# A fused linear layer with a low-rank update on one core: where three small software stores are issued, and which chunk's rows they carry

## The chip, the cores and the metric

The kernel runs on one core of one Trainium2 chip. The metric is the device time of a run in microseconds (us); the time of a kernel is the median of several runs. A profile is one execution, and its times count from the first instruction of its span.

## The reference

```python
x_flat = x.reshape(-1, in_dim)                 # x: 16 x 2048 x 256, so 32768 rows of 256
y = x_flat @ W                                 # W: 256 x 256
lora_out = x_flat @ lora_A                     # lora_A: 256 x 16
lora_out = lora_out * lora_E                   # lora_E: 16
lora_out = lora_out @ lora_B                   # lora_B: 16 x 256
y = y + scale * lora_out                       # scale = 1.0
return y.reshape(batch, seq_len, out_dim).astype(np.float32)
```

All inputs and the output are float32. The input x and the output y are 33.5 MB each. The low-rank factors can be multiplied out once, so that what is left is y = x (W + scale A E B).

## The kernel before

**Tiling.** The 32,768 rows are cut into 4 chunks of 8,192. A chunk lies in SBUF as 128 partitions x 64 rows x 256 columns: partition p of chunk c holds 64 rows that follow each other in memory, 64 KB. There are three homes for chunks (`home(c)`, L116), so chunk 3 uses the home of chunk 0. A result overwrites the input rows that it was computed from, and is stored from the same home.

**Groups.** The work goes by groups of 4 rows per partition: 16 groups in a chunk, 64 in all. Four engines pass each group on:

- GpSimd (POOL) casts 4 rows of a home to bf16 into `stage` (L191).
- TensorE (PE) transposes the stage, two bf16 taken as one fp32 word (`turn`, L242).
- VectorE (DVE) copies the transposed words from PSUM to `xt` (L226).
- PE multiplies by `weff`, the merged weight (`multiply`, L253).
- ScalarE (ACT) copies the product from PSUM back into the home (L207).

Stage, `xt` and both PSUM tiles have two buffers each. PE runs the loop of turn(i + 1) and multiply(i), so a turn runs one group ahead. After the last cast, GpSimd waits for the last turn but one, drains, and adds to one more stage semaphore (L193, L194), which releases the surplus turn at the end of PE's loop.

**Loads and stores.** `ORDER` (L18) lists by hand what SP issues, in order: "L" and "S" are a load and a store of rows s to e of a chunk. All of them go through SP's hardware queue (q1 in the profile). A store waits on `s_done`, which ACT raises behind a drain when a row group that ends a store is done (L210, L211). A load of chunk 3 waits until the store of chunk 0 has landed from the rows that it overwrites (L152).

**The shares.** One chunk, `SHARED`, has its first and last row in each partition left out of its hardware store. `share` (L161) stores these two rows, 1 KB each, from GpSimd's software queue (q0), in three DMAs, in the order of `SHARES` (L38): partitions 108 to 112 (5 of them, 10 KB), 0 to 107 (108, 216 KB) and 113 to 127 (15, 30 KB). Before the change SHARED is 1. The three DMAs raise one semaphore, `shared_stored`, and SP waits for all three at the end of its list (L159). That they may be issued is told by `s_shared`, which ACT raises behind a drain when it has written the last group of the shared chunk (L208, L209).

**The hold.** At chunk 2, row 16 (`HELD`, group 36), GpSimd does more than cast. First it waits for the load that brings these rows. Then it waits on `s_shared`, issues the three shares, and waits until the store of chunk 0, rows 0 to 39 (`HOLDERS`), has landed. Only then does cast 36 run.

**The end.** Behind SP's wait on L159 all engines meet in an exit barrier (L288, L324 in the profile), and after it SP waits for the three hardware stores (of chunks 1, 2 and 3) that nothing else waits for (`wait_for_stores`, L283; L284 in the profile).

Of the kernel before, what the change touches and what calls it, by code (L numbers as in the profile page):

```python
# [28 lines left out]
    ("S", 0, 40, 64),  # L29
    ("L", 3, 0, 32),  # L30
    ("L", 3, 32, 64),
    ("S", 1, 1, 63),
    ("S", 2, 0, 64),
    ("S", 3, 0, 64),
]

SHARED = 1
SHARES = (slice(108, 113), slice(0, 108), slice(113, P))  # L38

HELD = (2, 16)  # L40
# [14 lines left out]
def kernel(  # L55
# [45 lines left out]
    s_shared = sem("shared_done")  # L101
    shared_stored = sem("shared_stored")
# [13 lines left out]
    def home(c):  # L116
        return homes[c % N_HOMES]

    sync, gpsimd, scalar, vector, tensor = nc.sync, nc.gpsimd, nc.scalar, nc.vector, nc.tensor
# [41 lines left out]
    def share(engine, p, landed):  # L161
        first_and_last = (p, slice(0, ROWS, ROWS - 1))
        to, of = y_chunks[SHARED], home(SHARED)
        engine.dma_start(out=to[first_and_last], in_=of[first_and_last]).then_inc(landed, 16)  # L164

    def gpsimd_program():
        gpsimd.memset(ident[:], 0.0).then_inc(s_ident, 1)  # L167
        gpsimd.wait_ge(s_ident, 1)
        gpsimd.affine_select(  # L169
            out=ident[:],  # L170
            in_=ident[:],
            compare_op=ALU.not_equal,
            fill=1.0,
            base=0,
            pattern=[[-1, P]],
            channel_multiplier=1,
        ).then_inc(s_ident, 1)
        for g in range(N_GROUPS):
            c, b = g // GPC, g % GPC * CG
            for op, landed in loaded.items():  # L180
                if op[1:3] == (c, b):
                    gpsimd.wait_ge(landed, 16)
            if (c, b) == HELD:
                gpsimd.wait_ge(s_shared, 1)
                for p in SHARES:
                    share(gpsimd, p, shared_stored)
                for op in HOLDERS:
                    gpsimd.wait_ge(stored[op], 16)
            if g >= NS:
                gpsimd.wait_ge(s_turned, g - NS + 1)  # L190
            gpsimd.tensor_copy(out=stage[g % NS][:], in_=home(c)[:, b:b + CG, :]).then_inc(s_stage[g % UNROLL], 1)  # L191

        gpsimd.wait_ge(s_turned, N_GROUPS - NS + 1)  # L193
        gpsimd.drain().then_inc(s_stage[N_GROUPS % UNROLL], 1)  # L194

    def scalar_program():
        for name, to, of in (
            ("w", w_sb, W.rearrange("(q t) m -> q t m", t=KT)),
            ("b", b_sb, lora_B),
            ("e", e_sb, lora_E[:, None]),  # L200
        ):
            ins = scalar.dma_start(out=to[:], in_=of).then_inc(set_up_loaded[name], 16)
            opening.append(ins.ins.name)
        for g in range(N_GROUPS):
            c, b = g // GPC, g % GPC * CG
            scalar.wait_ge(s_y, g + 1)
            scalar.copy(out=home(c)[:, b:b + CG, :], in_=psum_y[g % NY][:]).then_inc(s_free[(g + NY) % UNROLL], 1)  # L207
            if (c, b + CG) == (SHARED, ROWS):  # L208
                scalar.drain().then_inc(s_shared, 1)  # L209
            if g in ends:  # L210
                scalar.drain().then_inc(s_done, 1)  # L211
# [76 lines left out]
    with tc.tile_critical(no_gpsimd_drain=True):  # L288
        sync_program()
        gpsimd_program()  # L290
        scalar_program()
        vector_program()
        tensor_program()
# [35 lines left out]
```

## Time and profile before

| what | value |
|---|---|
| median of 5 runs | 163.16 us (161.99 to 163.62) |
| the profiled execution | 161.78 us, its span 160.5 us |
| hardware queue q1 | 2304 packets, 66.86 MB |
| software queue q0 | 160 packets, 0.26 MB |
| GpSimd casts (L191) | 64 of 1040 ns |
| ACT copies (L207) | 64 of 1012 ns |
| GpSimd issues of a share (L164) | 3 of 674 ns |
| SP's issue of the last store | at 117.45 us |

How to read the profile: the page gives the busy time of each engine and its share of the span; then the span in 40 slices, one digit each, in tenths busy, with the load of the 16 DMA engines and their GB/s below; then the DMA queues with their packets and bytes. A line of a wait names who waited, for whom, and the us in total, the number of waits and the longest. A timeline line gives the start in us, the time taken, the engine, the line of the program, the operation and its tiles, and in brackets the idle time ahead of it and what ended it. The DMA view can be taken of a window: its 40 slices are then of that window, and the bytes of a packet are counted where it starts. SP's own work (issuing, waiting) is shown as SPq.

### The profile page before, as it was taken

How to read it: one execution, taken by the hardware profiler on the slowest of the kernel's cores; microseconds unless marked ns; L12 is line 12 of the kernel's file. 1: busy time of each engine (PE TensorE's matmuls, PEld its weight loads, DVE VectorE, ACT ScalarE, POOL GpSimd, SP SyncE). 2: the span in 40 equal slices, each digit the busy share in tenths (PEclk: the TensorE clock that was granted, in tenths of full speed). 3: DMA queues.
4: the chain of work that ended last, by engine and by line, in shares of the span. 5: the costliest groups of instructions: out<-in, count | busy, mean ns of one | idle time of the engine just before them, and what ended most of it. 6: DMA issues, size and time to landing. Idle time of an engine off the chain costs nothing.

```text
span 160.5 us, 2030 instructions
## 1 busy us (share of the span) xinstructions
PE 93.2 (58%) x782; PEld 81.9 (51%) x782; DVE 45.4 (28%) x66; ACT 66.1 (41%) x65; POOL 68.6 (43%) x73
## 2 busy tenths in 40 slices
PE   2979969959999990000999999999900000000000
PEld 1449958959999990000899989999800000000000
DVE  0155534525555550000255545555300000000000
ACT  3015775747777772000277777777720000000000
POOL 1527838377777734003577687687000000000000
PEclk9999999999999998555599999999995555555555
DMA  7999999999999997989999999979998998998993
GB/s 263 411 429 455 410 457 408 482 417 400 433 433 527 429 392 327 485 359 429 467 402 459 408 433 466 493 317 475 491 416 376 506 425 376 490 441 376 490 408 147
DMA packets 2675, 67.43 MB, mean 420 GB/s; under 512 B 528, under 2 KB 544, under 8 KB 752
## 3 DMA queue, kind: packets, MB, share of 16 engines
q1 hardware_dynamic: 2304, 66.86, 97.5%
q10 hardware_dynamic: 208, 0.28, 0.6%
q0 software_dynamic: 160, 0.26, 0.4%
q14 instruction: 3, 0.02, 0.0%
HBM read 33.85 MB, written 33.55 MB: 420 GB/s over the span
## 4 chain that ended last, share of the span: by engine, by line
DMA 42%; PE 26%; POOL 1%; ACT 1%; issue 1%; SPq 0%; ACTq 0%
DMA out_dram<-home 30%; PE psum_y L253 17%; DMA home<-in_x_dram 12%; PE psum_xt L242 9%; POOL stage L191 1%; ACT home L207 1%; SPq L153 0%; ACTq L211 0%; SPq L324 0%; SPq L288 0%
## 5 line engine op out<-in xcount | busy, mean ns | idle before, releaser
L207 ACT COPY home<-psum_y 128x1024 f32<-128x1024 f32 x64 | 64.8, 1012 | 49.3 <-PE psum_y L253 49.3
L191 POOL CAST stage<-home 128x1024 bf16<-128x1024 f32 x64 | 65.8, 1040 | 37.4 <-DMA home<-in_x_dram 14.5
L253 PE MATMUL psum_y<-weff,xt 128*128 128x256 bf16 x512 | 67.3, 275 | 0.0
L226 DVE COPY xt<-psum_xt 128x1024 bf16<-128x1024 bf16 x64 | 44.3, 692 | 61.8 <-PE psum_xt L242 61.8
L253 PEld LDWEIGHTS psum_y<-weff,xt 128*128 128x128 bf16 x512 | 50.7, 99 | 5.5
L242 PE MATMUL psum_xt<-ident,stage 128*128 128x128 f32 x260 | 40.8, 280 | 20.2 <-POOL stage L191 19.8
L242 PEld LDWEIGHTS psum_xt<-ident,stage 128*128 128x128 f32 x260 | 31.1, 144 | 23.1 <-issue 21.8
L266 PE MATMUL psum_y<-ident 128*128 128x512 f32 x4 | 3.8, 1101 | 2.9 <-POOL ident L169 2.9
L164 POOL DMA_DIRECT2D out_dram<-home x3 | 2.0, 674 | 4.5 <-DMA home<-in_x_dram 4.5
L266 PEld LDWEIGHTS psum_y<-ident 128*128 128x128 f32 x4 | 1.2, 323 | 3.9 <-POOL ident L169 2.9
L216 DVE TENSOR_SCALAR ate<-psum_y,e_sb 16x256 f32<-16x256 f32 x1 | 0.5, 472 | 7.2 <-PE psum_y L269 7.2
L207 ACT ACT_TABLE_LOAD x1 | 1.3, 1283 | 2.1 <-SPq L288 2.1
L275 PE MATMUL psum_y<-b_sb,ate 16*128 16x256 f32 x4 | 1.2, 416 | 0.0
L275 PEld LDWEIGHTS psum_y<-b_sb,ate 16*128 16x128 f32 x4 | 0.7, 202 | 0.4 <-issue 0.3
L167 POOL MEMSET ident<- 128x128 f32 x1 | 0.2, 204 | 1.7 <-SPq L288 1.7
L269 PEld LDWEIGHTS psum_y<-ident,a_sb 128*16 128x16 f32 x2 | 0.3, 137 | 1.2 <-issue 1.2
L230 DVE TENSOR_TENSOR weff<-w_sb,psum_y 128x512 bf16<-128x512 f32 x1 | 0.7, 689 | 0.5 <-PE psum_y L275 0.5
L269 PE MATMUL psum_y<-ident,a_sb 128*16 128x128 f32 x2 | 0.6, 421 | 0.0
L169 POOL TENSOR_SCALAR_AFFINE_SELECT ident<-ident 128x128 f32<-128x128 f32 x1 | 0.3, 283 | 0.2 <-POOL ident L167 0.2
L310 POOL MEMSET const-float32-0.0<- 128x1 f32 x1 | 0.1, 98 | 0.2 <-issue 0.2
L310 POOL MEMSET const-bfloat16-1.0<- 128x1 bf16 x1 | 0.1, 101 | 0.0
L310 POOL MEMSET const-uint8-127<- 128x1 uint8 x1 | 0.1, 101 | 0.0
(1 smaller groups left out, 0.1 us busy)
## 6 DMA issues: line engine op xcount, KB each, us to landing
home<-in_x_dram SPq DMA_DIRECT2D x4, 4096.0 KB, 24.8
out_dram<-home SPq DMA_DIRECT2D x1, 7936.0 KB, 38.6
home<-in_x_dram SPq DMA_DIRECT2D x3, 2048.0 KB, 13.2
home<-in_x_dram SPq DMA_DIRECT2D x1, 6144.0 KB, 57.3
out_dram<-home SPq DMA_DIRECT2D x1, 5120.0 KB, 48.1
home<-in_x_dram SPq DMA_DIRECT2D x1, 3072.0 KB, 20.0
out_dram<-home SPq DMA_DIRECT2D x1, 3072.0 KB, 46.2
home<-in_x_dram SPq DMA_DIRECT2D x1, 1024.0 KB, 5.3
```

The source lines that it names most:

```text
L164: engine.dma_start(out=to[first_and_last], in_=of[first_and_last]).then_inc(landed, 16)
L191: gpsimd.tensor_copy(out=stage[g % NS][:], in_=home(c)[:, b:b + CG, :]).then_inc(s_stage[g % UNROLL], 1)
L207: scalar.copy(out=home(c)[:, b:b + CG, :], in_=psum_y[g % NY][:]).then_inc(s_free[(g + NY) % UNROLL], 1)
L216: vector.tensor_scalar(out=ate[:], in0=psum_y[0][:R, :KT, :P], scalar1=e_sb[:], scalar2=float(scale), op0=ALU.mult, op1=ALU.mult,).then_in ...
L226: vector.tensor_copy(out=xt[g % NX][:], in_=psum_xt[g % NT][:].bitcast(BF16)).then_inc(s_xt[g % UNROLL], 1)
L230: vector.tensor_add(out=weff[:], in0=w_sb[:], in1=psum_y[1][:, :KT, :]).then_inc(s_free[0], 1)
L242: ins = tensor.transpose(psum_xt[i % NT][:, b, :], words[:, b, :], ident[:])
L253: ins = tensor.matmul(psum_y[i % NY][:, b, :], xt[i % NX][:, b, t::KT], weff[:, t, :], start=(t == 0), stop=(t == KT - 1),)
L266: tensor.matmul(psum_y[1][:, :2, :], ident[:], ident[:, None, :].to_broadcast([P, 4, P]), start=True, stop=True)
L269: ins = tensor.transpose(psum_y[0][:R, t, :P], a_sb[:, t, :], ident[:])
L275: ins = tensor.matmul(psum_y[1][:, t, :], ate[:, t, :], b_sb[:], start=True, stop=True)
L310: nc = _bacc.Bacc("TRN2", target_bir_lowering=False, num_devices=1)
```

## The change

The shared chunk becomes chunk 2. Chunk 1's hardware store carries all 64 rows of each partition, and chunk 2's rows 1 to 62. GpSimd no longer waits on `s_shared` and issues the shares in the hold ahead of cast 36; it does so after the last cast and after the drain that releases PE's last turn. At the hold the wait for the store of chunk 0 stays. ACT raises `s_shared` after the last group of chunk 2 (group 47) instead of chunk 1 (group 31), as L208 follows SHARED.

```diff
-    ("S", 1, 1, 63),
-    ("S", 2, 0, 64),
+    ("S", 1, 0, 64),
+    ("S", 2, 1, 63),
     ("S", 3, 0, 64),
 ]
 
-SHARED = 1
+SHARED = 2
 SHARES = (slice(108, 113), slice(0, 108), slice(113, P))
...
             if (c, b) == HELD:
-                gpsimd.wait_ge(s_shared, 1)
-                for p in SHARES:
-                    share(gpsimd, p, shared_stored)
                 for op in HOLDERS:
                     gpsimd.wait_ge(stored[op], 16)
...
         gpsimd.wait_ge(s_turned, N_GROUPS - NS + 1)
         gpsimd.drain().then_inc(s_stage[N_GROUPS % UNROLL], 1)
+        gpsimd.wait_ge(s_shared, 1)
+        for p in SHARES:
+            share(gpsimd, p, shared_stored)
```

## The prediction

> **What bounds the kernel now.** I read the page first for busy shares, then the slices, then the chain that ended last, then the waits of the issuing queues, then the DMA view in narrow windows around the two places that the change touches.
>
> ```profile
> span 160.5 us, 2030 instructions
> PE 93.2 (58%) x782; PEld 81.9 (51%) x782; DVE 45.4 (28%) x66; ACT 66.1 (41%) x65; POOL 68.6 (43%) x73
> POOL 1527838377777734003577687687000000000000
> DMA  7999999999999997989999999979998998998993
> q1 hardware_dynamic: 2304, 66.86, 97.5%
> q0 software_dynamic: 160, 0.26, 0.4%
> HBM read 33.85 MB, written 33.55 MB: 420 GB/s over the span
> ```
>
> No engine is busy for more than 58% of the span, and all of them stop three quarters of the way through, while the DMA line stays at 7 to 9 tenths until the last slice. The hardware queue's packets fill 97.5% of 16 engines' span. The 67.4 MB of traffic is the bound; what the shares carry is 0.26 MB of it. The waits of the queue on SP and of POOL show how little the engines' order decides:
>
> ```profile
> SPq L284 <- SPq L284: 41.0, 1, 41.0
> POOL stage L191 <- DMA out_dram<-home: 10.4, 1, 10.4
> POOL out_dram L164 <- DMA home<-in_x_dram: 4.5, 1, 4.5
> ```
>
> SP starts its last wait 41.0 us ahead of the end, at 119.4, when only stores are left. The last store was issued at 117.45 and took 0.33, so 1.65 us lie between it and this wait: the exit barrier. POOL's timeline shows the two idle stretches around the shares, and where its casts end:
>
> ```profile
> 62.49 2.02 POOL L164 DMA_DIRECT2D out_dram<-home  x3 [4.54 <-DMA home<-in_x_dram]
> 74.96 2.02 POOL L191 CAST stage<-home 128x1024 bf16<-128x1024 f32 x2 [10.45 <-DMA out_dram<-home]
> ...
> 111.60 1.04 POOL L191 CAST stage<-home 128x1024 bf16<-128x1024 f32 x1 [0.27 <-PE psum_xt L242]
> ```
>
> How long the shares take today, from the page's list of issues (last number: us from issue to landing), and the DMA view of 67.5 to 75, where their packets first appear (62.5 to 67.5 has none on q0):
>
> ```profile
> out_dram<-home POOLq DMA_DIRECT2D x1, 216.0 KB, 13.7
> out_dram<-home POOLq DMA_DIRECT2D x1, 30.0 KB, 14.9
> out_dram<-home POOLq DMA_DIRECT2D x1, 10.0 KB, 7.9
> ```
> ```profile
> q1 hardware_dynamic: 99, 3.09, 95.4%
> q0 software_dynamic: 99, 0.21, 7.1%
> ```
>
> Last, the DMA view of 155 to 160.5 in slices of 0.1375 us. A packet of 65,536 bytes in one slice reads 477 GB/s, so the line counts the starts of the last round of packets, one on each of the 16 engines:
>
> ```profile
> GB/s 0 477 0 0 0 0 0 0 953 1907 1430 953 477 477 0 477 477 0 0 477 0 0 0 0 0 0 0 0 0 0 0 0 0 0 0 0 0 0 0 0
> ```
>
> After the lone 477 at 155.2 (still the round before), the 16 starts lie between 156.1 and 157.7; their mean slice is number 11.2, the last is 19. The engine that ends last does so 7.8 slices, 1.07 us, after the mean one. That is all that a perfect balance at the end could give.
>
> **The change part by part.** The sum is made on the profiled execution (161.78 us, span 160.5), which lies 1.38 below the median of the five runs, 163.16; I carry the difference over.
>
> *The three issues leave the place ahead of cast 36* (chunk 2, row 16). They took 2.02 us on POOL, from 62.49 to 64.5. The cast behind them waits for the store of chunk 0's first 40 rows and starts at 74.96, so POOL stood idle for 10.4 us after them. Worth 0; the wait for that store is the cover, and without it 2.02 us of POOL would be gained. The wait for `s_shared` there goes too: ACT's drain for it (L209) started at 56.4 and took 1.04, so it was met before the load that POOL really waited for, at 62.49. Worth 0.
>
> *The share packets leave that store's time.* By 75, 0.21 of their 0.26 MB had been started. At the 423 GB/s of 62.5 to 74.9 that is 0.50 us by which the store may land earlier, and with it cast 36 and the issue of chunk 3's first load, both near 74.9. Neither sets the end: the load queues behind chunk 0's other store, and the last store, issued at 117.45, reaches the engines only when that of chunk 2 is through, 20.8 us of packets before the end (eight rounds of 2.42 plus the stagger), so at about 139. Late next is the queue itself. I take 0, bounds -0.5 and 0.
>
> *Two rows change places between the hardware stores.* Chunk 1's store grows from 7,936 to 8,192 KB, chunk 2's shrinks by the same. One ends 0.26 MB / 420 GB/s = 0.6 us later, the other then ends where it did. Both were issued well ahead (83.2 and 96.5). Net 0.
>
> *ACT's drain for `s_shared`* moves behind group 47, where L211 already drains (1.04). Two in a row cost 1.04 and 0.014 at the end of chunk 1 today, and one of each will stay. Net 0.
>
> *The shares now go out behind the last cast.* The cast ends at 112.64, the drain that releases PE's last turn comes before them (L194: 313 ns from 112.9, done at 113.2), and `s_shared` is long set. Three issues of 0.674 take until about 115.3. Nothing that computes is queued behind them on POOL; the exit barrier is. On SP, L159 now waits for their landing, with the exit barrier (1.65) and the last wait queued behind it, and the program's end behind that. So: when do they land? First packets came 5.0 us after the first issue: 118.2 now. From there to the last landing (63.9 + 14.9 = 78.8) were 11.3 us. Software packets took turns with hardware packets of 41 KB (1.97 MB in 48 packets of the window 62.5 to 67.5, 91.1% of 16 x 5 us: 1.52 each), later 24 KB ones of about 0.9: 4.6 turns of 1.6 to 74.9, then about 4 of 1.0, so nine turns. Now the packets beside them are of 63 to 66 KB: 263 of them in 118 to 160.5 at 93.5% of 16 x 42.5 us, 2.42 each, 2.5 with the software packet. Nine turns are 22.5 us: landing at about 141. With a third more turns it is 148. SP's last wait is released at 160.4; take 1.65 off for the barrier and 10 us are left at the worse of these. I take 0, bounds 0 and +3.3 (first rival).
>
> *The bytes on each engine* stay as they were: the three issues keep order and size. But 20 KB or so more on a late engine is 20 KB / 27 GB/s (65.5 KB in 2.42 us) = 0.76 us, and the order in which engines leave the last loads decides who is late. Bounds -1.07 (balanced) and +0.8; I take 0, as the total per engine is nearest to the row of before.
>
> A rule against the change, to be left out by whoever wants rows alone: the Trainium skill, "DMA: Bandwidth & Descriptors", gives about 2.0 us fixed for each software DMA (section "Anatomy of one DMA") and calls DMAs under 64 KB mostly overhead ("Rules for kernel authors"); two of these three are 10 and 30 KB. By it, estimated, three fixed costs at the open end would be +6 us, about 169; the rows above put the whole landing 10 us or more inside other transfers, and by them it is 0.
>
> Sum: 161.78 + 0 = 161.78, and 163.16 + 0, rounded **163.2 us**. A difference of about 1% (1.63 us) is what a measurement of this kernel can tell from no change; the five runs of before spread over 1.63.
>
> **The rivals.**
>
> *The shares land last (slower).* Place: L159 on SP. If each 1 KB row were a packet of its own, the 108-partition share would need 18 turns on an engine where 9 partitions go through it, and all three some 23: 118.2 + 23 x 2.5 = 175.7. It decides from (160.1 - 118.2) / 2.5 = 17 turns on. The price has a cap, as the last store leaves the engines at 160.1 and the rest then runs alone: six packets of up to 4 KB at 27 GB/s, 0.15 each, 0.9; 0.4 of landing as for the last store; 1.65 of barrier; near 3.3 with what is left between: 166.5. For it: every small packet has to wait behind a 2.42 us one. Against: 160 packets for 256 KB and 48 completions mean that rows travel together, and nine turns sufficed before.
>
> *The middle gets smoother and the end evener (faster).* The slices from 60.2 and 64.2 show 7 tenths and 327 to 485 GB/s around the old issue. Between 58.5 and 62.5 the rate is 360 against 420: 4 us x 60/420 = 0.6. If the shares caused that and went from the end's imbalance as well, 0.6 + 1.07 = 1.67: 161.5 us. Against: the dip starts before the first issue at 62.49, and 104 to 108, with no share near, shows 333.
>
> *The early landing carries through (no change still).* If the 0.5 us were kept to the end: 162.7.
>
> *The other order leaves the late engine later (no change still).* +0.8: 164.0.
>
> **How the numbers follow.** No change in the mean, in its three forms, 0.83: its own range is 163.2 - 1.07 to 163.2 + 0.8, 162.1 to 164.0. Shares landing last 0.06, and 0.04 for a late engine beyond 0.8 with a partial delay: slower 0.10. The smoother middle 0.05, and 0.02 for both bounds below at once: faster 0.07. The own range holds about 7 in 10; moved out to the 1% bounds on either side, 161.5 to 164.8, it holds a little over 8 in 10, and the first rival lies outside.
>
> **What would show it.** POOL: no L164 at 62.5, three at about 113.3, and an idle wait of about 12 us ahead of cast 36 for the store alone. DMA: no q0 packets at 67 to 79, all 160 between 118 and 141 (148 at most). SP: the last wait begins at about 142 instead of 119.4, and lasts about 18 us instead of 41. The store of chunk 0 lands up to 0.5 us earlier, with the last store's issue up to 0.5 earlier and the span's end unmoved. The prediction is wrong if SP's last wait is short or gone, if L159 ends after 158, or if the last round of packets is spread over much more or less than 1.6 us.

## The result and the profile after

| | before | after |
|---|---|---|
| median | 162.34 us (79 runs, 161.5 to 163.73) | 161.22 us (42 runs, 160.74 to 162.36) |
| profiled execution | 161.78 us, span 160.5 us | 161.13 us, span 159.8 us |

The ratio after to before is 0.9937, with a 95% interval of 0.9923 to 0.9951: the change saves 0.63%, 1.02 us of 162.34. (It is the ratio of the means, 161.34 to 162.37; that of the medians is 0.9931.) The median of before was 163.16 in the five runs that the prediction was made from, and is 162.34 over 79.

The page of the changed kernel, with the same lines as for before:

```profile
span 159.8 us, 2029 instructions
PE 94.5 (59%) x782; PEld 82.8 (52%) x782; DVE 45.4 (28%) x66; ACT 66.1 (41%) x65; POOL 68.9 (43%) x73
DMA  6999999999999997989999999979979979979976
q1 hardware_dynamic: 2304, 66.86, 97.9%
q0 software_dynamic: 160, 0.26, 0.4%
```

Packets and bytes are the same, and the DMA engines are still the bound. The waits of SP and POOL, and POOL's timeline:

```profile
SPq L144 <- DMA out_dram<-home: 22.3, 1, 22.3
SPq L284 <- SPq L284: 17.7, 1, 17.7
POOL stage L188 <- DMA out_dram<-home: 16.9, 1, 16.9
```
```profile
74.72 2.02 POOL L188 CAST stage<-home 128x1024 bf16<-128x1024 f32 x2 [16.85 <-DMA out_dram<-home]
...
114.03 2.02 POOL L164 DMA_DIRECT2D out_dram<-home  x3 [1.04 <-PE psum_xt L242]
```

The first line is SP at the end of its list, waiting for the shares (the wait of L159, which the view puts under L144): 22.3 us from 118.1 to 140.4. After the exit barrier it still waits 17.7 us for the last hardware store, so the shares do not set the end. Their landing, from the page's list of issues:

```profile
out_dram<-home POOLq DMA_DIRECT2D x1, 216.0 KB, 21.0
out_dram<-home POOLq DMA_DIRECT2D x1, 30.0 KB, 25.0
out_dram<-home POOLq DMA_DIRECT2D x1, 10.0 KB, 7.3
```

The software packets start between 119.5 and 140.1, in nine bursts about 2.4 us apart, which is the time of one of the 65,536-byte packets beside them (2.42 us).

The last round of packets, in the DMA view of 155 to 160.5 (477 GB/s is one packet's start in a slice of 0.1375 us):

```profile
GB/s 0 0 0 0 0 0 477 953 953 0 953 2860 953 0 477 0 0 0 0 0 0 0 0 0 0 0 0 0 0 0 0 0 0 0 0 0 0 0 0 0
```

The mean start is in slice 10.0, the last in 14: 0.55 us apart, where it was 1.07 before. In this pair of executions half a microsecond of the 0.65 is there. The experiments test whether the gain rests on that.

### The profile page after: what moved, and what is told of

It reads as the page before. It is cut to its first block, busy times and chain, and to the rows that moved or that the text cites. A ratio compares the mean times of both kernels' runs of the same rounds, so it can differ in the third digit from the quotient of the medians.

```text
span 159.8 us, 2029 instructions
## 1 busy us (share of the span) xinstructions
PE 94.5 (59%) x782; PEld 82.8 (52%) x782; DVE 45.4 (28%) x66; ACT 66.1 (41%) x65; POOL 68.9 (43%) x73
## 3 DMA queue, kind: packets, MB, share of 16 engines
q1 hardware_dynamic: 2304, 66.86, 97.9%
## 4 chain that ended last, share of the span: by engine, by line
DMA 42%; PE 26%; POOL 1%; ACT 1%; SPq 1%; issue 0%; ACTq 0%; POOLq 0%
DMA out_dram<-home 30%; PE psum_y L253 17%; DMA home<-in_x_dram 13%; PE psum_xt L242 9%; POOL stage L188 1%; ACT home L207 1%; SPq L153 0%; ACTq L211 0%; SPq L324 0%; POOLq L187 0%; SPq L288 0%
## 5 line engine op out<-in xcount | busy, mean ns | idle before, releaser
L253 PE MATMUL psum_y<-weff,xt 128*128 128x256 bf16 x512 | 69.0, 280 | 0.0
L253 PEld LDWEIGHTS psum_y<-weff,xt 128*128 128x128 bf16 x512 | 51.4, 100 | 6.3
```

The lines of the kernel that those rows point to most:

```text
L253: ins = tensor.matmul(psum_y[i % NY][:, b, :], xt[i % NX][:, b, t::KT], weff[:, t, :], start=(t == 0), stop=(t == KT - 1),)
```

## Where the packets take longer

Three views of the kernel before give a measure that the page's slices are too coarse for. First a calm stretch, 20 to 40, loads alone; then 79 to 83, where the engines go over from chunk 0's stores to chunk 3's loads; then 99 to 103, where they go over to chunk 1's store:

```profile
q1 hardware_dynamic: 304, 8.65, 100.2%
...
q1 hardware_dynamic: 79, 1.73, 102.9%
...
q1 hardware_dynamic: 50, 1.61, 100.4%
```

The last number is the time that the packets took, as a share of 16 engines in the window; a packet counts whole where it starts, so it can pass 100%. In the calm stretch that is 1.002 x 16 x 20 / 8.65 = 37.1 us of one engine per MB. At the first switch it is 38.1, at the second 39.9. Over what the bytes take at the calm rate (37.06 before rounding), the two windows cost each engine 0.11 and 0.29 us. The same two windows of the changed kernel:

```profile
q1 hardware_dynamic: 77, 1.76, 102.4%
...
q1 hardware_dynamic: 49, 1.74, 105.9%
```

That is 37.2 and 39.0 us per MB, 0.02 and 0.21 us. I call the sum of both the excess at the switches (before 0.40, after 0.23) and give it for the runs below, as one profile of each can say only so much.

A longer packet at a change of direction is not in itself a sign of the shares. The change from loads to chunk 0's stores, in the window 58 to 76, first for before and then for after, has more of it than either switch:

```profile
q1 hardware_dynamic: 211, 6.89, 92.4%
...
q1 hardware_dynamic: 223, 7.18, 97.2%
```

That is 38.6 and 39.0 us per MB, an excess of 0.67 and 0.87 us: as much without early shares as with them, so it is left out of the sum.

## The experiments

Every run was timed beside runs of the kernel before on the same chip. Four theories come up: A, the shares even out the end (it takes four engines to get 4 KB of shares, twelve to get 20 KB, and the four to be late; the profile does not name the engine of a packet, so this was not seen); B or E, software packets early in the run cost by themselves; C, the choice of rows matters; D, engines put apart ahead of the switches cost. N, that software packets close ahead of the first switch cost, came later.

**Place alone.** The shares stay with chunk 1.

```diff
             if (c, b) == HELD:
-                gpsimd.wait_ge(s_shared, 1)
-                for p in SHARES:
-                    share(gpsimd, p, shared_stored)
...
         gpsimd.drain().then_inc(s_stage[N_GROUPS % UNROLL], 1)
+        gpsimd.wait_ge(s_shared, 1)
+        for p in SHARES:
+            share(gpsimd, p, shared_stored)
```

> The shares stay with chunk 1's rows, and only their place moves behind the last cast. Theory A (balance: the shares give 4 of the 16 DMA engines about 4 KB and 12 of them 20 KB; given behind the last loads, the 4 light ones are those that are late by then, so the last round ends more evenly): ratio to before 0.994, last round of packets spread over about 1.1 us as after the change instead of 1.5. Theory B (what is saved is the early place itself, in the hold and beside chunk 0's stores): 0.994 too. Theory C (which chunk's rows go through the software queue is what counts): 1.000.

Measured: 0.9942 (0.991 to 0.9975), excess 0.05. C is out: the gain is in the place. But the last packet started about 1.0 us behind the mean one, as in before, and the gain was there all the same.

**No shares at all.**

```diff
-    ("S", 1, 1, 63),
+    ("S", 1, 0, 64),
...
-        sync.wait_ge(shared_stored, 16 * len(SHARES))
...
-                gpsimd.wait_ge(s_shared, 1)
-                for p in SHARES:
-                    share(gpsimd, p, shared_stored)
```

> No software stores at all: the hardware stores of chunks 1 and 2 carry all 64 rows. Theory A: without the relief the late engines stay late by the 16 KB (0.6 us) that the light ones are spared, so no better than before: 0.999 to 1.004, and the last packet starts 1 us or more after the mean one. Theory B: nothing early is left to pay for, 0.994. Theory C: 1.000.

Measured: 0.9952 (0.9922 to 0.9982), excess 0.11. Its last round, in the same window and slices as above:

```profile
GB/s 0 0 0 0 0 1430 953 0 1907 477 953 0 0 1430 0 477 0 0 0 0 0 0 0 477 0 0 0 0 0 0 0 0 0 0 0 0 0 0 0 0
```

One engine starts last in slice 23, 1.8 us behind the mean of the round. This execution took 162.32, more than the kernel's median of 161.75, so its uneven end may well have cost it something. The ratio is what speaks against A, which had 0.999 to 1.004: without any shares the kernel is 0.5% faster, so those of before were not worth having, and A is out as the main cause. What shares in the late place give on top, 0.9937 against 0.9952, is inside the intervals.

**Late, with another four engines light.**

```diff
 SHARED = 2
-SHARES = (slice(108, 113), slice(0, 108), slice(113, P))
+SHARES = (slice(113, P), slice(0, 108), slice(108, 113))
```

> As after the change, but the shares of 15 and 5 partitions change places in the order of issue (15, 108, 5), which should put the 4 light engines elsewhere among the 16. Theory A: the late engines now get 20 KB instead of 4, 0.6 us more, so most of the gain goes: 0.998 to 1.002, the spread of the last round 1.5 us or more. Theory B and C: 0.994, as after the change.

Measured: 0.9951 (0.9922 to 0.9979), excess 0.05. B's number, 0.994, is inside the interval; A's range begins at 0.998, just outside it.

**Issued ahead of chunk 3's first cast**, chunk 1's rows.

```diff
+            if (c, b) == (3, 0):
+                gpsimd.wait_ge(s_shared, 1)
+                for p in SHARES:
+                    share(gpsimd, p, shared_stored)
             if (c, b) == HELD:
-                gpsimd.wait_ge(s_shared, 1)
-                for p in SHARES:
-                    share(gpsimd, p, shared_stored)
```

> Chunk 1's rows, issued ahead of chunk 3's first cast (near 93 us), so that the first software packets start near 98, at the end of the last loads (their last round starts near 99 to 100.7). Theory A: most turns still come after the last loads: 0.995, between 0.993 and 0.998. Theory B, if the hold and chunk 0's stores are what the early place costs: 0.994; if it is being ahead of the last loads: 0.997 to 1.000.

Measured: 0.9917 (0.9887 to 0.9948), excess 0.08. No cost in this place either.

**The old place, even shares.**

```diff
-SHARES = (slice(108, 113), slice(0, 108), slice(113, P))
+SHARES = (slice(0, P),)
```

> The place of before (in the hold, chunk 1's rows), but one software DMA of all 128 partitions, 16 KB on every engine, instead of 4 KB on four and 20 KB on twelve. Theory D (the uneven bytes, put ahead of the last loads, leave the engines staggered there, which costs 0.5 to 1 us by the end): 0.994, like the kernel without shares. Theory E (software packets early in the run cost by themselves, wherever they fall among the engines): 1.000. Theory A (balance at the end) would give 0.999 to 1.004.

Measured: 0.9973 (0.9944 to 1.0001), excess 0.16. Between D and E: the interval just misses D's 0.994 and just holds E's 1.000.

**The old place, twice the shares.** `share` takes the rows as an argument; chunk 1's hardware store is left with rows 2 to 61.

```diff
-    ("S", 1, 1, 63),
+    ("S", 1, 2, 62),
...
-                for p in SHARES:
-                    share(gpsimd, p, shared_stored)
+                for rows in (slice(0, ROWS, ROWS - 1), slice(1, ROWS - 1, ROWS - 3)):
+                    for p in SHARES:
+                        share(gpsimd, p, shared_stored, rows)
```

> The place of before, but four rows of each partition (0, 1, 62, 63) through the software queue in six DMAs: 8 KB on the four light engines, 40 KB on the other twelve, 1.2 us apart. Theory D: the cost doubles, 1.004 to 1.008. Theory E, if it is the turns of the software queue: 1.004 to 1.006; if it is one fixed cost: 1.000. If the early shares are harmless: 1.000 or below.

Measured: 1.0041 (1.0016 to 1.0067). Its two windows, 79 to 83 and 99 to 103:

```profile
q1 hardware_dynamic: 68, 1.42, 92.0%
...
q1 hardware_dynamic: 54, 1.73, 116.0%
```

41.5 and 42.9 us per MB: an excess of 0.39 and 0.63, 1.02 in all. More early shares, more time, and more of it at the switches.

**The same place in the code, behind the wait for the store.**

```diff
             if (c, b) == HELD:
+                for op in HOLDERS:
+                    gpsimd.wait_ge(stored[op], 16)
                 gpsimd.wait_ge(s_shared, 1)
                 for p in SHARES:
                     share(gpsimd, p, shared_stored)
-                for op in HOLDERS:
-                    gpsimd.wait_ge(stored[op], 16)
```

> Chunk 1's rows, the three shares issued after the wait for chunk 0's store instead of ahead of it, so near 74.7; cast 36 starts 2.0 us later, with some 20 us of slack behind it. The software packets take their turns from 80 on, beside the end of chunk 0's second store and the first load of chunk 3, still ahead of the last loads. Theory D: 1.000, as the stagger is still there before the last loads. Theory E, if it is the issue at the change from loads to stores near 62 that costs: 0.994.

Measured: 0.9944 (0.9919 to 0.9968), excess 0.07. POOL issued the shares at 75.58 instead of 62.49, and cast 36 came 2.0 us behind them:

```profile
75.58 2.02 POOL L164 DMA_DIRECT2D out_dram<-home  x3 [17.39 <-DMA out_dram<-home]
77.59 2.03 POOL L191 CAST stage<-home 128x1024 bf16<-128x1024 f32 x2
```

Thirteen microseconds of delay, the same bytes, the same engines, and the whole gain. It also shows that the 2.02 us on POOL, now uncovered, cost nothing. The windows of 79 to 83 and 99 to 103:

```profile
q1 hardware_dynamic: 74, 1.67, 97.4%
...
q1 hardware_dynamic: 51, 1.67, 97.7%
```

37.3 and 37.4 us per MB, next to nothing beyond the calm rate.

**The kernel before, once more.**

> The kernel before, once more, as a second profile of it and as a measure of how far two sets of runs of one program differ: 1.000, within 0.003.

Measured: 1.0006 (0.9978 to 1.0034), excess 0.40 again.

**The early rows by the hardware queue, uneven and even.** SP issues them between chunk 0's second store and chunk 3's first load; GpSimd issues none.

```diff
-SHARES = (slice(108, 113), slice(0, 108), slice(113, P))
+SHARES = (slice(0, 108), slice(108, P))
...
             kind, c, s, e = op
+            if op == ("L", 3, 0, 32):
+                sync.wait_ge(s_done, 3)
+                for p in SHARES:
+                    share(sync, p, shared_stored)
```

> The first and last rows of chunk 1 go out early, but through SP's hardware queue, between chunk 0's second store and chunk 3's first load, as two DMAs of 108 and 20 partitions. If 108 partitions go by 12 engines and 20 by 10, the engines are left 18 to 22 KB (0.7 to 0.8 us) apart from the four that get none, just ahead of the switch from stores to loads. Theory D (the stagger ahead of the switch is what costs): 1.000, from 0.998 to 1.004. Theory E (software packets early): 0.994 to 0.996.

Measured: 0.9963 (0.9937 to 0.9988), excess at the second switch 0.07 (the first window holds the 1 KB rows themselves, so it is not comparable). The two DMAs left 22 completions in the trace (2,582 packets on the hardware queue against 2,304, of which 256 are the rows), where the even form below left 16; 12 and 10 engines, as expected, would leave 22.

The even form has `SHARES = (slice(0, P),)`.

> The same place and queue as the hardware run with two DMAs, but one DMA of all 128 partitions, 16 KB on each engine. Theory D: 0.995, like the kernel without shares. Theory E: 0.995 as well. If rows of 1 KB cost ahead of the switch however they are issued: 1.000.

Measured: 0.9939 (0.991 to 0.9968), excess at the second switch 0.19. The intervals of the two overlap. D's 1.000 is outside that of the uneven one, the lower end of its range, 0.998, inside: rows that should put the engines apart just ahead of the switch cost less than the software shares of before, if anything.

**The old place, twice the shares, even**: the doubled run with `SHARES = (slice(0, P),)`.

> The place of before, four rows of each partition through the software queue as in the doubled run, but as two DMAs of 128 partitions, 32 KB on each engine. Theory D: 0.995 to 0.998, as the engines are not moved apart. Theory E (software turns early in the run): 1.002 to 1.005, close to the doubled run with uneven shares (1.0041).

Measured: 0.9971 (0.9947 to 0.9996), excess 0.61. Even shares in the old place give the same time, once or twice, within these intervals. So here the time follows neither the number of turns nor the excess (0.16 and 0.61).

**The old place, another four engines light**: before with `SHARES = (slice(113, P), slice(0, 108), slice(108, 113))`.

> The place of before, with the shares of 15 and 5 partitions exchanged in the order of issue, so that another four engines are the light ones. Theory D in its plain form (any four engines 16 KB ahead of the others at the switch): 1.000. If it matters that the light ones of before are late by something else: 0.996 to 0.998, or 1.003, as the others are nearer to or farther from the rest. Theory E: 1.000.

Measured: 1.0008 (0.9981 to 1.0034), excess 0.84. The order of issue, and with it which engines should be light, makes no difference to the time that these runs can tell.

**Earlier and later within the hold.** Issued ahead of the wait for chunk 2's second load:

```diff
+            if (c, b) == HELD:
+                gpsimd.wait_ge(s_shared, 1)
+                for p in SHARES:
+                    share(gpsimd, p, shared_stored)
             for op, landed in loaded.items():
                 if op[1:3] == (c, b):
                     gpsimd.wait_ge(landed, 16)
             if (c, b) == HELD:
-                gpsimd.wait_ge(s_shared, 1)
-                for p in SHARES:
-                    share(gpsimd, p, shared_stored)
```

> As before, but the three shares are issued ahead of the wait for chunk 2's second load, near 58 instead of 62.5, so that their packets (from 63 to about 75) are through some 5 us ahead of the switch from stores to loads at 80, with the engines just as far apart. Theory D (engines apart at the switch): 1.000. Theory N (software packets in the last few us ahead of the switch lengthen the packets at it): 0.994 to 0.996.

Measured: 0.9976 (0.9946 to 1.0005), excess 0.80. The last software packet started at 76.5.

And about 6 us later, behind five more casts of group 36, which only let time go by:

```diff
                 gpsimd.wait_ge(s_shared, 1)
+                gpsimd.wait_ge(s_turned, g - NS + 1)
+                for again in range(5):
+                    gpsimd.tensor_copy(out=stage[g % NS][:], in_=home(c)[:, b:b + CG, :]).then_inc(s_again, 1)
+                    gpsimd.wait_ge(s_again, again + 1)
                 for p in SHARES:
```

> As before, but GpSimd first casts group 36 five times more (about 6 us, only to pass time, in its idle stretch), so that the shares are issued near 68.7 and their packets run from about 73.7 to 85, across the switch at 80. Theory D: between the place of before and that behind the hold, 0.997 to 1.000. Theory N: 1.000 or above.

Measured: 0.9988 (0.9958 to 1.0019), excess 0.40. Issued at 68.64, with packets from 73.1 to 82.2. Neither place is clear of before's 1.000, and the intervals of the two overlap. That of the early one also reaches down to N's 0.996, and that of the late one holds N's 1.000. So the times do not decide about N. The excess does not either, as it differs between executions: the three profiles of 161.8 to 162.1 us (before, before again, at 68) have 0.40 each, the two of 162.9 and 163.0 (at 58, other engines) 0.80 and 0.84, and the ratios of before and of the other engines are the same.

**Twice the shares, behind the wait for the store**: the doubled run with the order of the run behind the wait.

> Four rows of each partition, uneven as in the doubled run, issued behind the wait for chunk 0's store. Theory D: the switch from stores to loads is past, but the engines are 32 KB (1.2 us) apart at the last switch near 100: 0.996 to 1.000. Theory N: software packets beside loads are harmless at twice the number too: 0.994.

Measured: 0.995 (0.992 to 0.9979), excess 0.12. In the place behind the wait even the double amount costs nothing that these runs can tell.

**Twice the shares, behind the last cast**: the changed kernel with rows 0, 1, 62 and 63.

```diff
-    ("S", 2, 1, 63),
+    ("S", 2, 2, 62),
...
+        for rows in (slice(0, ROWS, ROWS - 1), slice(1, ROWS - 1, ROWS - 3)):
+            for p in SHARES:
+                share(gpsimd, p, shared_stored, rows)
```

> The changed kernel with four rows of each partition of chunk 2 (0, 1, 62, 63) issued behind the last cast. Theory A in a weak form (the light engines are late by about one share): 0.994 to 0.998, as two shares make the other twelve late. If the light engines are late by more than one share: 0.991. Theories D and N: 0.994, as nothing follows but stores.

Measured: 1.009 (1.0055 to 1.0125), so 1.009 / 0.9937 = 1.5% or 2.5 us above the changed kernel. No theory had expected this. SP's waits and the end of the chain say why:

```profile
SPq L144 <- DMA out_dram<-home: 41.8, 1, 41.8
```
```profile
113.72 0.05 POOLq L191
113.77 0.75 issue
114.52 3.91 POOL out_dram L164 x6
```

The last wait for the hardware stores is gone from the list; SP waits 41.8 us for the shares, to about 160.4, and the exit barrier comes behind that, to a span of 162.4. The shares now land last. This is the prediction's first rival, brought about by twice the turns.

**The two best again, side by side.** First the kernel with the shares ahead of chunk 3's first cast, then the changed kernel.

> The kernel with chunk 1's shares issued ahead of chunk 3's first cast, run again beside the changed kernel, since it had the lowest ratio so far (0.9917, against 0.9937 of the change). If the place beside the last loads is better than that behind the last cast: 0.992, and 0.002 or more below the changed kernel of the same runs. If it is only one of the places that come after the costly stretch: 0.994, within 0.002 of it.

Measured: 0.9926 (0.9903 to 0.9949), excess 0.09.

> The changed kernel again, as the measure for the run beside it and as its second profile: 0.994. In the trace, packets beyond their usual time at the two switches near 80 and 100 add up to under 0.3 us per engine, as in every run without early software packets so far.

Measured: 0.9934 (0.9901 to 0.9967), excess 0.11. 0.0008 apart, so the same: no version was found that beats the changed kernel.

**What the runs say together.**

| software packets | runs: ratio (excess at the switches, us) |
|---|---|
| start before 80, uneven | before 1 (0.40); again 1.0006 (0.40); other engines 1.0008 (0.84); at 58 0.9976 (0.80); at 68 0.9988 (0.40); double 1.0041 (1.02) |
| start before 80, even | 0.9973 (0.16); double 0.9971 (0.61) |
| start behind 80, or none | after 0.9937 (0.23), again 0.9934 (0.11); place alone 0.9942 (0.05); none 0.9952 (0.11); other engines 0.9951 (0.05); ahead of chunk 3's casts 0.9917 (0.08), again 0.9926 (0.09); behind the wait 0.9944 (0.07), double 0.995 (0.12) |

Shown by the times: the cost of the old place comes from software stores that are on the DMA engines during chunk 0's stores, from 67.5 to 79 in before, ahead of chunk 3's loads, and it vanishes when the same stores go out after 80. Uneven ones cost more than even ones in the middle of their intervals. (The single shares issued at 68 run on to 82.2, the doubled uneven ones to 92.1.) Shown by the profiles: the packets at the two switches take longer in those runs. For the five profiles of single uneven early shares the excess is 0.57 us on average, for the eight single runs in the last row 0.10. Their profiled times differ by 0.90 us (162.33 against 161.43), so about half of the difference is found at the switches. The other half is at the end of the run as far as the profiles tell: the last packet starts 1.4 us behind the mean of its round in the five, and 1.0 in the eight. Both halves are averages over executions that vary: the end alone from 0.7 to 1.9 us in the five and from 0.4 to 1.7 in the eight. For the one pair of before and after, the hardware packets take the same time over the whole span (97.5% of 160.5 and 97.9% of 159.8, 156.5 and 156.4 us on each engine), and the half microsecond at the end is most of it.

Not settled: why load and store packets at 80 and at 100 get longer after software stores at 63 to 79. Engines standing apart is not enough (the runs without shares and behind the wait had first loads 1.2 and 1.3 us apart, against 0.7 and 1.1 in the two profiles of before, and no cost). Software packets as such are not enough (those at 80 to 92, ahead of the second switch, were free). Whether nearness to the first switch counts (N) the runs at 58 and 68 do not decide. Why the last round was evener in the late runs is open too, and so is whether the software queue matters: the rows went by the hardware queue only near 81 to 82, never at 63 to 79.

## Why the prediction was wrong

- **The bound and the path** were right: 97.9% of 16 engines' span on the hardware queue, and no computing engine near the end.
- **The issues on POOL at 0**: right, and shown with the cover taken away: behind the wait, cast 36 came 2.0 us later and nothing was lost.
- **The landing of the shares**: right in each number. First packets about 5.4 us after the issue at 114.03, nine turns, last landing 115.5 + 25.0 = 140.5 (predicted about 141); SP's last wait 17.7 us (predicted about 18). The issue came 0.7 later than predicted. The idle time ahead of cast 36 is 16.85 and not about 12, as the timeline now counts the load's wait in the same gap.
- **"The share packets leave that store's time... I take 0, bounds -0.5 and 0"**: this is the step that failed. It priced the early share packets by their bytes and by the landing of one store, found both off the path, and so let them cost nothing. Cast 36 did come 0.24 us earlier, and the last store was issued at about 117.8, 0.3 later, both without effect on the end. But the packets in the old place cost about 1.0 us in all, by the times: moved away or left out, they gave ratios of 0.9917 to 0.9952. The term should have been -1.02. In the averages of the profiles about half of that is longer packets at the two switches; by the shares' bytes alone it can't be seen. The working let bytes move at one rate all along the span. The windows at the two switches show 38.1 and 39.9 us per MB against 37.1, and that row could have been read beforehand, though it would not have told what caused it.
- **"The bytes on each engine stay as they were... I take 0"**: the totals did. The profiled end was 0.5 us evener, inside the bound of -1.07. How much of the gain that is stays open: the place alone gained as much by its median, with an end as uneven as before's in its profile (1.0 us), but on average the late runs have the evener end. Of the signs that were named for being wrong, this is the one that came near: the starts of the last round are spread over 1.1 us, not 1.6.
- **"Two rows change places" and ACT's drain at 0**: nothing contradicts them; the place alone gave 0.9942 and the whole change 0.9937.
- **The rivals.** "The middle gets smoother and the end evener" had the right sign, at 0.05, and half of its place. The dip that it named, 58.5 to 62.5, stayed: 360 GB/s after the change as before, and the first software packet of before came only at 67.5. (Its row was also misread: of the slices from 60.2 and 64.2 only the first shows 7 tenths, the second shows 9.) Its other half, the evener end, came in the profiles. I dismissed it because 104 to 108 is slow as well without a share near, which was no argument, since what is slowed need not be near. "The shares land last" was rightly held to be unlikely for three shares; with six it came true, at 2.5 us against a cap of 3.3.
- **The level**: 0.82 us of the miss in microseconds is the reference itself, whose median went from 163.16 in five runs to 162.34. Carrying the ratio of 0.9937 to 163.16 gives 162.1, the lower edge of the likeliest case's own range; the measured 161.22 lies below that range, and below 161.5. That about 1% is what a measurement can tell from no change was too coarse: with 79 and 42 runs, 0.63% is clear of it.
- **The rule on small software DMAs** (the Trainium skill, "DMA: Bandwidth & Descriptors", "Anatomy of one DMA"): the estimate of 6 us that the prediction made from its fixed cost did not come. The shares landed at 140.5, and the last hardware store kept SP waiting for 17.7 us more behind the barrier. In the doubled run, where the shares do end last, the whole price was 2.5 us.

## What to carry to other kernels

In a kernel that keeps all DMA engines full, "the same bytes in another place" is not free by itself: compare the engine time per MB in the windows where the traffic changes direction with that of a calm stretch, and suspect small side transfers that run ahead of such a change. Then move them or leave them out and time it, as the largest excess here (58 to 76) had nothing to do with them. A trick that was meant to balance the queues should be timed against leaving it out; here leaving it out was 0.5% faster. Beside packets of 2.42 us the small queue here got one turn in each 2.4 us, nine for the three shares, so count such turns against what is left of the run before putting more into it.

## What the runs showed that I had not expected

- The three software stores of before, 0.4% of the bytes, cost 0.5% against none (0.9952), and nothing that the runs could tell in any place from 80 us on that left them time to land.
- Landing last is not far off: the shares of the change left 17.7 us to spare, and twice as many made the run 2.5 us longer.
- Even early shares gave the same time, within the intervals, at 16 KB and at 32 KB on each engine (0.9973 and 0.9971).
